# Attention steps, gate steps and accumulating loads set to other times in an fp32 encoder layer, with branch A's operands fetched in ten loads instead of sixteen

## The chip, the cores and the metric

The kernel runs on one core of one Trainium2 chip. The metric is the device time of one execution in microseconds (us), as the median of three runs. Steps, pairs and engines are named as in the program: PE is the matrix engine, DVE the vector engine, ACT the scalar engine, POOL GpSimd, and SP the engine that issues most DMAs.

## The reference

One encoder layer on x of 512 tokens by 2048 channels, fp32. The normed input h goes through one combined projection, whose columns feed a sparse attention (branch A, 8 heads of 128, with a learned top-k key choice), a retention (branch B, 8 heads of 128) and two sigmoid merge gates. Each branch is multiplied by a SiLU gate, projected to 2048 channels, gate-merged, projected once more and added to x; a small gated projection of p and a last norm follow.

```python
a = dsa_mixer(...) * silu(gate_a)          # gate_a, gate_b: columns of the combined projection
b = retention_mixer(...) * silu(gate_b)
merged = sigmoid(g_a) * (a @ w_a) + sigmoid(g_b) * (b @ w_b)
x = x + merged @ w_o
```

## The kernel before

**Products.** An fp32 product is made from two fp32r parts of each operand: a high part, which ACT copies off (`wh`, line 176), and a low part, which DVE subtracts (`wl`, line 183). Weights arrive as raw tiles through SP (line 150). Where a raw tile must hold the sum of two weight blocks, POOL adds the second block with an accumulating DMA (`add_block`, line 137), or DVE adds two raw tiles (line 185).

**A pair** (`gemm_pair`) makes two output blocks with seven products instead of eight, n = 0 to 6, into four banks: `ps_v`, `ps_p`, `ps_q`, `ps_r`, `ps_p`, `ps_v`, `ps_p`. A bank that is used again has to be copied off first: ACT copies `pv` after n = 0, `e1` after n = 1, `e2` after n = 4 and `e3` after n = 6 (line 279), and DVE makes the four results `e_t` (line 283). So product n = 4 waits for `e1`, and product n = 6 for `e2`. A pair has 112 matmuls and a step every two of them, 56 steps. The pairs of `w_b` are short, with four k blocks instead of eight and 28 steps, and use half-size raw tiles (`half_raws`). A plain `gemm` has 24 matmuls and a step every three.

**Order.** Every engine works its instructions off in program order. The program lays the order down by hand: `later(n, f)` issues f n steps on, and `step` runs what is due between two matmuls. A step set later thus puts its instruction behind others on that engine.

**Stages around the change**, in microseconds of the profile: four pairs for branch B's SiLU gate and three for half of branch A's, to about 945, with POOL adding the results (`gate_pair` with `adder=pool`, line 1004) and ACT taking the SiLU one step after (line 1051 and POOL's product and store, lines 1052 and 1053; for branch A line 1013 with its store in line 1014). Then eight pairs for q and k of the attention heads, to about 1165, one per head. The steps of head h are issued during the next two pairs, by the list `steps` in `attention_head`: logits and their maxima, `exps` (DVE `nm` in line 1107, ACT line 1110), `normalize` (DVE lines 1114 and 1118, ACT line 1120), the transposes of the probabilities on PE (`turn`, line 1129), their high parts `pth` and `p3` (ACT, lines 1135 and 1138) and low parts `ptl` (DVE, line 1143), the products with the values (`outs`, lines 1155 and 1157), and the store of the head. One more gate pair lies ahead of the projection of branch B: six plain blocks of `w_b`, four short pairs, two plain blocks. Its operands `bk` are loaded during that last gate pair and split into parts (lines 847 and 848). The result of a short pair is added by POOL (line 1264), multiplied by the merge gate on DVE and stored by SP (lines 1260 and 1261). Branch A's operands for the projection by `w_a`, which begins at about 1278, are loaded by `a_load`, multiplied by their gate on POOL (line 1229) and split.

Of the kernel before, what the change touches and what calls it, by code (L numbers as in the profile page):

```python
# [34 lines left out]
def block_kernel(tc, xT, pT, posb, posq, w_in, w_v, w_k, w_a, w_b, w_o, w_ple, w_gate,  # L35
# [4 lines left out]
    with contextlib.ExitStack() as ctx:  # L40
# [94 lines left out]
        def add_block(r, b):  # L135
            src, k0 = b
            pool.dma_start(out=raw_tiles[r], in_=src[:, k0:k0 + raws[r][2], :], accum_op=OP.add)  # L137

        def load_to(n):
            need = max((u[0] for u in units[:n]), default=-1) + 1  # L140
            while state["raw"] < need:
                i = state["raw"]
                src, k0, nk, cols, plus = raws[i]
                if nk * cols <= L and i < 4:
                    t = U("wraw4").rearrange("p (a c) -> p a c", c=128)
                elif i in half_raws:
                    t = shared("raw", F32, "wraw", RAW_BUFS)
                else:
                    t = wp.tile([128, 8, 128], F32, name="wraw", tag="wraw", bufs=RAW_BUFS)
                sp.dma_start(view(t, nk, cols), src[:, k0:k0 + nk, :])  # L150
                raw_tiles[i] = t
                if plus is not None:
                    add_block(i, plus)
                state["raw"] += 1

        def split_to(n):
# [43 lines left out]
        def later(n, f):  # L200
            if n <= 0:
                return f()
            tick[1] += 1
            heapq.heappush(soon, (tick[0] + n, tick[1], f))
# [791 lines left out]
        def gate_pair(ids, finish, wide=256, adder=None):  # L996
            t = B("go")
            outs = [t[:, 0:512], t[:, 512:1024]]
            have = [0, 0]

            def done(c0, c1, i, q):
                o = outs[i]
                to = alt(o, q)[:, 4 - wide // 64:, :]
                (adder or dve).tensor_add(to, fit(c0, to), fit(c1, to))  # L1004
                have[i] += 1
                if have[i] == 2:
                    later(1, lambda: finish(i, o))

            gemm_pair(ids, Xh, done, wide=wide)

# [51 lines left out]
        def attention_head(h):  # L1062
# [61 lines left out]
            def turn(i):  # L1124
                ps = E["pt", i] = P("ps_pt")
                js = [(0, t) for t in range(4)] if i == 0 else [(1, 1), (1, 2), (1, 3), (3, 3)] if i == 1 \
                    else [(2, 2), (2, 3)]
                for n, (j, t) in enumerate(js):
                    pe.transpose(ps[:, tok(n)], E["bm"][:, TOFF[t] + 128 * j:TOFF[t] + 128 * j + 128], ident)

            def high(i):
                if i == 0:
                    E["p"] = B("pth", F32R), B("ptl", F32R)
                n = (512, 384, 256)[i]
                act.activation(E["p"][0][:, JOFF[i]:JOFF[i] + n], E["pt", i][:, 0:n], AF.Copy)
                if i == 1:
                    E["p3"] = U("p3")
                    act.activation(E["p3"][:, 0:128], E["pt", i][:, 384:512], AF.Copy)

            def low(i):  # L1140
                n = (512, 384, 256)[i]
                c = slice(JOFF[i], JOFF[i] + n)
                dve.tensor_sub(E["p"][1][:, c], E["pt", i][:, 0:n], E["p"][0][:, c].bitcast(F32))
# [4 lines left out]
            def outs(n):  # L1148
                if n == 0:
                    E["po"] = P("ps_o")  # L1150
                po = E["po"]
                for i in range(3 * n, min(3 * n + 3, len(seq))):
                    a, b, j = seq[i]
                    if j == NT - 1:
                        pe.matmul(po[:, 384:], E["v"][0][:, tok(3)].bitcast(F32), E["p3"][:, 0:128], start=False, stop=False)
                    else:
                        pe.matmul(po[:, 128 * j:], E["v"][a][:, tok(j)], E["p"][b][:, JOFF[j]:JOFF[j] + L - 128 * j],
                                  start=(i == 0), stop=(i == len(seq) - 1))
                if n == 3:
                    E["oT"] = U("oT")  # L1160
                    act.activation(E["oT"], po, AF.Copy)

            def store():
                sp.dma_start(od[h], E["oT"])

            steps = [(-30, loads), (-8, mask), (30, values_load)]
            steps += [(n, lambda t=t: logits(t)) for t, n in enumerate((20, 22, 24, 26))]
            steps += [(28, exps), (34, normalize)]
            steps += [(50, lambda i=i: turn(i)) for i in range(3)]
            steps += [(n, lambda i=i: high(i)) for i, n in enumerate((52, 52, 54))]  # L1170
            steps += [(n, lambda i=i: low(i)) for i, n in enumerate((54, 54, 56))]
            steps += [(n, lambda i=i: outs(i)) for i, n in enumerate((65, 65, 69, 69))]
            steps += [(73 + STORE_LAG // 2, store)]
            return done, steps

        for n in range(Z_FIRST):
# [42 lines left out]
        def b_load(h):  # L1219
            t = U("bk")  # L1220
            sp.dma_start(t, bd[h])
            bk[h] = t
            later(25 if h < 5 else 44 - 3 * h + 4 * (h - 5), lambda: bparts.append(split(t, "b", 1)))

        def a_load(h):
            t, z = U("ak"), U("z")
            sp.dma_start(t, od[h])
            sp.dma_start(z, zd[h])
            later(25, lambda: pool.tensor_mul(z, z, t))
            later(29, lambda: aparts.append(split(z, "a", 1)))  # L1230

        for n in range(Z_FIRST, NH // 2):
            if n == NH // 2 - 1:
                for h in range(NH):
                    later(4 + 3 * h, lambda h=h: b_load(h))
            gate_pair(u_az[n], to(zd[2 * n:2 * n + 2], AF.Silu), adder=pool)

        gates = {}
# [13 lines left out]
            later(4, lambda: sp.dma_start(mbs[m], s))  # L1252

        def project_two(m):
            t = U("bo"), U("bo")
            have = [0, 0]

            def finish(i):
                s = gates.pop(m + i)
                dve.tensor_mul(s, t[i], s)  # L1260
                later(8, lambda: sp.dma_start(mbs[m + i], s))

            def done(c0, c1, i, q):
                pool.tensor_add(t[i][:, q], c0, c1)
                have[i] += 1
                if have[i] == 2:
                    later(8, lambda: finish(i))

            gate_load(m + 2)
            gate_load(m + 3)  # L1270
            gemm_pair(u_wb[m], Xb, done, order=range(4))
# [4 lines left out]
        for m in range(16):  # L1276
            if m < B_PAIRS or m >= B_PAIRS + 8:
                project_b(m)
            elif m % 2 == 0:
                if m == B_PAIRS + 4:  # L1280
                    for h in range(NH):
                        later(11 + 4 * h, lambda h=h: a_load(h))
                project_two(m)


# [336 lines left out]
B_PAIRS = 6  # L1622
# [101 lines left out]
```

## Time and profile before

| | |
|---|---|
| median of 3 runs | 1717.44 us (1717.02 to 1718.31) |
| the profiled execution | 1717.35 us, span 1715.5 us, mean granted clock 0.989 |
| PE busy | 1661.2 us, 97% of the span |
| DVE, ACT, POOL busy | 1413.2, 963.7, 350.8 us |
| mean DMA rate | 223 GB/s |

A time in the trace counts from the start of the span. What the program runs outside the span is the difference of the two, 1.85 us. PE's idle time is 54.3 us in all (1715.5 less 1661.2). The granted clock is the share of full speed that PE was given.

### The profile page before, as it was taken

The numbers are of one execution on the slowest core, as the hardware profiler recorded it, in microseconds if no ns is written. First come the engines' busy times: TensorE is split into PE (matmuls) and PEld (weight loads), VectorE is DVE, ScalarE is ACT, GpSimd is POOL, SyncE is SP. The second block draws the span as 40 slices with busy tenths as digits, with TensorE's granted clock in tenths as the row PEclk, the third lists the DMA queues.
The fourth block names the chain that finished last, engine by engine and source line by source line (L and its number), as shares of the span: only waits on it lengthen the run. The fifth ranks groups of instructions, "written<-read, shape, count | busy, mean of one in ns | idle before, by whom it ended". The sixth has DMA issues, their size and how long they took to land.

```text
span 1715.5 us, 26592 instructions
## 1 busy us (share of the span) xinstructions
PE 1661.2 (97%) x9632; PEld 1466.4 (85%) x9632; DVE 1413.2 (82%) x2257; ACT 963.7 (56%) x1501; POOL 350.8 (20%) x355
## 2 busy tenths in 40 slices
PE   9999999999999999999989999998889999999998
PEld 7999998888888888888778888887668888888897
DVE  8789887888988889888886767678687888899895
ACT  6556666555555555554445655556344445477673
POOL 3011111111111111113443101115350033311211
PEclk9999999999999999999999999999999999999999
DMA  8779888787887887878879888776777689998873
GB/s 295 262 237 249 207 207 209 198 218 173 229 225 179 233 225 172 238 202 215 208 184 225 233 231 189 215 203 211 210 275 245 179 224 293 275 321 228 226 236 128
DMA packets 144163, 382.19 MB, mean 223 GB/s; under 512 B 15648, under 2 KB 30112, under 8 KB 144032
## 3 DMA queue, kind: packets, MB, share of 16 engines
q1 hardware_dynamic: 106528, 261.20, 43.6%
q0 software_dynamic: 29872, 106.44, 34.5%
q10 hardware_dynamic: 7632, 12.85, 2.1%
q8 instruction: 76, 1.25, 0.3%
q14 instruction: 55, 0.45, 0.1%
HBM read 331.28 MB, written 49.15 MB: 222 GB/s over the span
## 4 chain that ended last, share of the span: by engine, by line
PE 75%; DVE 10%; issue 5%; ACT 4%; DMA 3%; POOL 2%; SPq 1%; ACTq 0%; POOLq 0%; DVEq 0%
PE ps_p L319 26%; PE ps_v L319 17%; PE ps_r L319 8%; PE ps_q L319 8%; DVE wl L183 4%; PE ps_vn L720 3%; PE ps_w L239 2%; PE ps_w L240 2%; PE ps_w L238 2%; ACT wh L176 1%; DMA wraw<-w_b 1%; POOL go L1004 1%; DVE e_t L283 1%; DVE isc L768 1%; DMA wraw<-w_in 1%
## 5 line engine op out<-in xcount | busy, mean ns | idle before, releaser
L183 DVE TENSOR_TENSOR wl<-wraw,wh 128x1024 fp32r<-128x1024 f32 (+1 forms) x521 | 623.4, 1202 | 189.8 <-ACT wh L176 186.6
L176 ACT ACTIVATE wh<-wraw 128x1024 fp32r<-128x1024 f32 (+2 forms) x520 | 522.8, 1016 | 288.2 <-DVE wraw L185 148.1
L137 POOL DMA_DIRECT2D wraw<-w_in x141 | 125.3, 922 | 805.0 <-DVE wl L183 346.2
L319 PE MATMUL ps_p<-hs,wh 128*128 128x512 f32 (+1 forms) x752 | 188.3, 392 | 0.0
L279 ACT ACTIVATE e<-ps_p 128x512 f32<-128x512 f32 (+1 forms) x195 | 115.0, 590 | 120.7 <-PE ps_p L319 115.6
L319 PEld LDWEIGHTS ps_p<-hs,wh 128*128 128x128 f32 x752 | 135.4, 190 | 24.0 <-issue 1.2
L319 PE MATMUL ps_p<-hs,wl 128*128 128x256 f32 (+1 forms) x752 | 111.8, 290 | 20.5 <-ACT e L279 15.4
L319 PEld LDWEIGHTS ps_p<-hs,wl 128*128 128x128 f32 x752 | 99.8, 196 | 24.0 <-ACT e L279 17.0
L319 PE MATMUL ps_r<-hs,wh 128*128 128x512 f32 (+1 forms) x376 | 98.6, 397 | 7.5 <-ACT wh L176 7.5
L319 PE MATMUL ps_p<-ha,wh 128*128 128x512 f32 (+1 forms) x376 | 95.4, 391 | 0.0
L319 PE MATMUL ps_v<-ha,wh 128*128 128x512 f32 (+1 forms) x376 | 92.9, 388 | 0.0
L319 PE MATMUL ps_v<-hs,wh 128*128 128x512 f32 (+1 forms) x376 | 92.2, 387 | 0.0
L319 PE MATMUL ps_q<-ha,wh 128*128 128x512 f32 (+1 forms) x376 | 92.1, 386 | 0.0
L319 PEld LDWEIGHTS ps_r<-hs,wh 128*128 128x128 f32 x376 | 68.1, 191 | 19.6 <-ACT wh L176 8.5
L319 PEld LDWEIGHTS ps_q<-ha,wh 128*128 128x128 f32 x376 | 70.2, 188 | 14.0 <-ACT wh L176 0.3
L319 PEld LDWEIGHTS ps_v<-hs,wh 128*128 128x128 f32 x376 | 70.3, 188 | 13.8
L319 PEld LDWEIGHTS ps_v<-ha,wh 128*128 128x128 f32 x376 | 69.7, 188 | 13.1
L185 DVE TENSOR_TENSOR wraw<-wraw 128x1024 f32<-128x1024 f32 (+1 forms) x65 | 77.5, 1193 | 2.2
L319 PEld LDWEIGHTS ps_p<-ha,wh 128*128 128x128 f32 x376 | 67.3, 189 | 11.6 <-ACT wh L176 0.4
L283 DVE TENSOR_TENSOR e_t<-ps_p,pv 128x512 f32<-128x512 f32 (+1 forms) x59 | 40.2, 681 | 30.7 <-ACT e L279 28.4
L720 PE MATMUL ps_vn<-wh,hh 128*128 128x296 f32 (+1 forms) x192 | 62.6, 331 | 0.6 <-DVE wh L174 0.4
L720 PE MATMUL ps_vn<-wh,hl 128*128 128x296 f32 (+1 forms) x192 | 62.2, 329 | 0.0
(451 smaller groups left out, 3605.8 us busy)
## 6 DMA issues: line engine op xcount, KB each, us to landing
wraw<-w_in SPq DMA_DIRECT2D x192, 512.0 KB, 4.9
wraw<-w_in POOLq DMA_DIRECT2D x141, 512.0 KB, 7.6
wraw<-w_o SPq DMA_DIRECT2D x32, 512.0 KB, 6.8
wraw<-w_o POOLq DMA_DIRECT2D x24, 512.0 KB, 7.4
wraw<-w_gate SPq DMA_DIRECT2D x24, 512.0 KB, 6.4
wraw<-w_gate POOLq DMA_DIRECT2D x18, 512.0 KB, 6.5
wraw<-w_a SPq DMA_DIRECT2D x16, 512.0 KB, 6.0
rl<-rr SPq DMA_DIRECT2D x24, 256.0 KB, 6.0
```

The lines of the kernel that those rows point to most:

```text
L137: pool.dma_start(out=raw_tiles[r], in_=src[:, k0:k0 + raws[r][2], :], accum_op=OP.add)
L176: act.activation(h, raw, AF.Copy)
L183: dve.tensor_sub(l, raw, h.bitcast(F32))
L185: dve.tensor_add(raw, raw, view(raw_tiles[plus], nk, cols))
L238: pe.matmul(o, h[:, k, w], a, start=(s == order[0]), stop=False)
L239: pe.matmul(o, h[:, k, w], b, start=False, stop=False)
L240: pe.matmul(o, l[:, k, w], a, start=False, stop=(s == order[-1]))
L279: act.activation(E[n], src, AF.Copy)
L283: f(t, x, y)
L319: pe.matmul(to, w[:, k], x, start=(n < 4 and part == parts[0] and k == order[0]), stop=(part == parts[1] and k == order[-1]), skip_group_c ...
L720: pe.matmul(pss[t], x[:, tok(t)], w[:, k], start=(s == 0 and n < NT * len(run) and x is a and w is h), stop=(s == KT - 1 and x is b))
L768: dve.match_replace(out=a, in_to_replace=m8, in_values=a, imm_value=-3.39e38)
```

## The change

The same instructions are issued at other steps, apart from the loads and products of branch A's operands.

- `add_block` of a short pair's raw tile comes 16 steps behind the load of that tile, where it followed at once.
- With `adder=pool`, the SiLU comes 16 steps behind its sum instead of one.
- In attention, `exps`, `normalize`, the transposes, their parts, `outs` and the store come 4 to 11 steps later.
- The product of a head with its SiLU gate moves into attention for heads 0 to 5: a load of the gate, and POOL's product ahead of the store. `a_load` then fetches one tile for these heads, and two for heads 6 and 7: ten loads of 256 KB instead of sixteen, one head every 10 steps from the first short pair on, and split during the last plain blocks of `w_b`.
- Branch B's operands are loaded and split earlier, and the product of a short pair with its merge gate comes 20 steps behind its sum instead of 8.

```diff
-                    add_block(i, plus)
+                    later(16 if i in half_raws else 0, lambda i=i, plus=plus: add_block(i, plus))
...
-                    later(1, lambda: finish(i, o))
+                    later(16 if adder else 1, lambda: finish(i, o))
...
+            def z_load():
+                if h < 2 * Z_FIRST:
+                    E["z"] = U("z")
+                    sp.dma_start(E["z"], zd[h])
+
+            def gate():
+                if h < 2 * Z_FIRST:
+                    pool.tensor_mul(E["oT"], E["z"], E["oT"])
...
-            steps += [(28, exps), (34, normalize)]
-            steps += [(50, lambda i=i: turn(i)) for i in range(3)]
-            steps += [(n, lambda i=i: high(i)) for i, n in enumerate((52, 52, 54))]
-            steps += [(n, lambda i=i: low(i)) for i, n in enumerate((54, 54, 56))]
-            steps += [(n, lambda i=i: outs(i)) for i, n in enumerate((65, 65, 69, 69))]
-            steps += [(73 + STORE_LAG // 2, store)]
+            steps += [(33, exps), (44, normalize)]
+            steps += [(54, lambda i=i: turn(i)) for i in range(3)]
+            steps += [(n, lambda i=i: high(i)) for i, n in enumerate((56, 56, 58))]
+            steps += [(n, lambda i=i: low(i)) for i, n in enumerate((58, 58, 60))]
+            steps += [(n, lambda i=i: outs(i)) for i, n in enumerate((69, 69, 73, 73))]
+            steps += [(48, z_load), (77, gate), (92, store)]
...
-            later(25 if h < 5 else 44 - 3 * h + 4 * (h - 5), lambda: bparts.append(split(t, "b", 1)))
+            later(26 + h if h < 3 else 40 - h, lambda: bparts.append(split(t, "b", 1)))
...
-            t, z = U("ak"), U("z")
+            t = U("ak")
             sp.dma_start(t, od[h])
-            sp.dma_start(z, zd[h])
-            later(25, lambda: pool.tensor_mul(z, z, t))
-            later(29, lambda: aparts.append(split(z, "a", 1)))
+            if h >= 2 * Z_FIRST:
+                z = U("z")
+                sp.dma_start(z, zd[h])
+                later(26, lambda: pool.tensor_mul(t, z, t))
+            later(112 + 1 + 2 * h - 10 * h, lambda: aparts.append(split(t, "a", 1)))
...
-                    later(4 + 3 * h, lambda h=h: b_load(h))
+                    later(2 + h if h < 3 else 3 * h - 1, lambda h=h: b_load(h))
...
-                    later(8, lambda: finish(i))
+                    later(20, lambda: finish(i))
...
-                if m == B_PAIRS + 4:
+                if m == B_PAIRS:
                     for h in range(NH):
-                        later(11 + 4 * h, lambda h=h: a_load(h))
+                        later(10 * h, lambda h=h: a_load(h))
```

On ACT, in the second half of the pair that follows a head's own, the order before is this. Line 1110 is the head's exponentials, line 1120 its normalization, `e2` the copy that product n = 6 of the running pair waits for, and `wh` a weight's high part.

```order
L1110 ACTIVATE bm_10360,sums_10247<-bm_10360,nm_10629 128x512
L176 ACTIVATE wh_10647<-wraw_10284 128x1024
L1120 ACTIVATE bm_10360<-bm_10360,ri_10655 128x128
L1120 ACTIVATE bm_10360<-bm_10360,ri_10655 128x256
L1120 ACTIVATE bm_10360<-bm_10360,ri_10655 128x384
L279 ACTIVATE e2_10673<-ps_p_10497 128x512
```

The same stretch of ACT in the change:

```order
L176 ACTIVATE wh_10643<-wraw_10284 128x1024
L1110 ACTIVATE bm_10360,sums_10247<-bm_10360,nm_10648 128x128
L1110 ACTIVATE bm_10360,sums_10247<-bm_10360,nm_10648 128x256
L1110 ACTIVATE bm_10360,sums_10247<-bm_10360,nm_10648 128x384
L1110 ACTIVATE bm_10360,sums_10247<-bm_10360,nm_10648 128x512
L279 ACTIVATE e2_10670<-ps_p_10495 128x512
L176 ACTIVATE wh_10672<-wraw_10502 128x1024
L1120 ACTIVATE bm_10360<-bm_10360,ri_10685 128x128
```

The copy `e2` and a weight's high part now stand ahead of the normalization, and another weight's high part ahead of the exponentials.

On DVE, at the end of that pair and the start of the next, the order before is this. `ptl` are the low parts of the transposed probabilities, `e_t` and `ak` belong to the k of the next head.

```order
L848 TENSOR_TENSOR aql_10707<-aq_10605,aqh_10706 128x512
L1143 TENSOR_TENSOR ptl_10732<-ps_pt_10712,pth_10731 128x512
L1143 TENSOR_TENSOR ptl_10732<-ps_pt_10717,pth_10731 128x384
L1143 TENSOR_TENSOR ptl_10732<-ps_pt_10722,pth_10731 128x256
L283 TENSOR_TENSOR e_t_10751<-ps_p_10497,pv_10528 128x512
L1085 TENSOR_TENSOR ak_10753<-e_t_10751 128x4x64
L283 TENSOR_TENSOR e_t_10755<-ps_r_10500,e3_10749 128x512
L1085 TENSOR_TENSOR ak_10753<-e_t_10755 128x4x64
L183 TENSOR_TENSOR wl_10765<-wraw_10570,wh_10764 128x1024
```

DVE in the change:

```order
L848 TENSOR_TENSOR aql_10712<-aq_10608,aqh_10711 128x512
L283 TENSOR_TENSOR e_t_10752<-ps_p_10495,pv_10530 128x512
L1085 TENSOR_TENSOR ak_10754<-e_t_10752 128x4x64
L283 TENSOR_TENSOR e_t_10756<-ps_r_10498,e3_10750 128x512
L1085 TENSOR_TENSOR ak_10754<-e_t_10756 128x4x64
L183 TENSOR_TENSOR wl_10766<-wraw_10566,wh_10765 128x1024
L1143 TENSOR_TENSOR ptl_10745<-ps_pt_10727,pth_10744 128x512
L1143 TENSOR_TENSOR ptl_10745<-ps_pt_10732,pth_10744 128x384
L848 TENSOR_TENSOR akl_10774<-ak_10754,akh_10773 128x512
L1143 TENSOR_TENSOR ptl_10745<-ps_pt_10737,pth_10744 128x256
```

The three `ptl` have moved behind two `e_t`, two `ak` and a weight's low part.

On SP, in the short pairs of `w_b`, the order before is this. `wraw` are weight loads, `sg` gate loads, and `mbs` the stores of results: those of line 1252 are of plain blocks, those of line 1261 of the first short pair.

```order
L1252 DMA mbs_1542<-sg_12560 128x512
L150 DMA wraw_12749<-w_b 128x512 x2
L150 DMA wraw_12781<-w_b 128x512 x2
L1243 DMA sg_12845<-sgb_1540 128x512
L1243 DMA sg_12847<-sgb_1540 128x512
L150 DMA wraw_12868<-w_b 128x512 x2
L1261 DMA mbs_1542<-sg_12621 128x512
L150 DMA wraw_12901<-w_b 128x512
L1261 DMA mbs_1542<-sg_12683 128x512
L150 DMA wraw_12901<-w_b 128x512
```

SP in the change, where `ak` are the loads of branch A's operands:

```order
L150 DMA wraw_12768<-w_b 128x512 x2
L1236 DMA ak_12792<-od_1180 128x512
L150 DMA wraw_12801<-w_b 128x512 x2
L1236 DMA ak_12827<-od_1180 128x512
L1254 DMA sg_12867<-sgb_1540 128x512
L1254 DMA sg_12869<-sgb_1540 128x512
L1236 DMA ak_12879<-od_1180 128x512
L150 DMA wraw_12891<-w_b 128x512 x2
L1236 DMA ak_12914<-od_1180 128x512
L150 DMA wraw_12923<-w_b 128x512 x2
L1236 DMA ak_12961<-od_1180 128x512
L1273 DMA mbs_1542<-sg_12638 128x512
```

The first short pair's stores have moved behind all loads of the short pairs, and five loads of branch A's operands stand among those.

More of the change, by code (lines that the diff above doesn't have):

```diff
@@ L1254, in project_two @@
         def project_two(m):
-            t = U("bo"), U("bo")
+            o = B("bo")
+            t = o[:, 0:512], o[:, 512:1024]
             have = [0, 0]
```

## The prediction

> **What bounds the kernel now.** I read the page first.
>
> ```profile
> span 1715.5 us, 26592 instructions
> PE 1661.2 (97%) x9632; PEld 1466.4 (85%) x9632; DVE 1413.2 (82%) x2257; ACT 963.7 (56%) x1501; POOL 350.8 (20%) x355
> ```
>
> PE is busy for 97% of the span, and the change leaves its matmuls as they are. All it can give back is the time in which PE waits, or in which it runs at a lower granted clock. The busy times of the four stretches that the change touches come next.
>
> ```profile
> core 0: us, PE busy (x) PEld busy (x) DVE busy (x) ACT busy (x) POOL busy (x), PEclk, DMA share, GB/s
> 780.00:945.00 165.00, 152.29 (x856) 131.86 (x855) 130.98 (x210) 76.62 (x99) 68.76 (x67) 0.99 0.82 211
> 945.00:1170.00 225.00, 209.64 (x1191) 186.88 (x1190) 158.33 (x266) 137.99 (x248) 30.17 (x33) 0.96 0.81 223
> 1170.00:1209.00 39.00, 37.03 (x160) 30.49 (x159) 31.77 (x49) 19.93 (x47) 21.34 (x23) 0.96 0.55 156
> 1209.00:1285.00 76.00, 61.23 (x303) 51.37 (x302) 59.56 (x71) 32.72 (x54) 36.92 (x32) 0.93 0.77 242
> ```
>
> They are the SiLU pairs, attention, the plain blocks of `w_b`, and the short pairs up to the start of `w_a`. PE is idle for 12.7, 15.4, 2.0 and 14.8 us in them (length less busy). The clock costs more: length times (1 less PEclk) gives 1.7, 9.0, 1.6 and 5.3 us. So the stakes are 14.4, 24.4, 3.5 and 20.1 us, 62.4 in all, and 1655 is the floor of what this change could reach. The waits say who holds PE up. In the SiLU pairs:
>
> ```profile
> ACT go L1051 <- POOL go L1004: 35.9, 8, 6.4
> ACT go L1013 <- POOL go L1004: 18.0, 6, 6.4
> PE ps_r L319 <- ACT wh L176: 7.5, 5, 2.0
> PE ps_p L319 <- DVE wl L183: 4.6, 7, 1.3
> ```
>
> ACT stands for 54 us at SiLUs whose sum POOL has not made, and the weights' high parts behind it come late to PE, and through them the low parts. In attention:
>
> ```profile
> PE ps_p L319 <- ACT e L279: 15.4, 8, 2.9
> DVE wl L183 <- ACT wh L176: 58.8, 33, 3.3
> POOL wraw L137 <- DVE wl L183: 141.4, 15, 21.4
> ```
>
> All of PE's waiting there is one wait per pair, for `e2` ahead of product n = 6. The timeline of one pair shows why, and what follows it (the last row is the busy-times view of the four microseconds after the wait).
>
> ```profile
> 974.58 1.26 PE L1129 MATMUL ps_pt<-cs,bm 128*128 128x128 f32 x10
> ...
> 993.70 0.40 ACT L1110 ACTIVATE bm<-bm,nm 128x128 f32<-128x128 f32 x1 [2.90 <-DVE nm L1107]
> ...
> 995.51 1.98 PE L319 MATMUL ps_v<-ha,wh 128*128 128x512 f32 x8
> ...
> 995.90 1.04 ACT L176 ACTIVATE wh<-wraw 128x1024 fp32r<-128x1024 f32 x1
> ...
> 998.38 1.30 ACT L1120 ACTIVATE bm<-bm,ri 128x128 f32<-128x128 f32 x3 [1.44 <-DVE ri L1114]
> 999.59 0.57 ACT L279 ACTIVATE e<-ps_p 128x512 f32<-128x512 f32 x1
> ...
> 1000.22 0.74 PE L319 MATMUL ps_p<-hs,wl 128*128 128x256 f32 x4 [1.78 <-ACT e L279]
> 1000.80 2.21 PE L1129 MATMUL ps_pt<-cs,bm 128*128 128x128 f32 x10
> ...
> 1000.20:1004.20 4.00, 3.98 (x20) 3.89 (x21) 3.02 (x4) 2.57 (x4) 1.42 (x2) 0.59 0.18 70
> ```
>
> ACT idles 1.44 us for the reciprocal, normalizes for 1.30 us, and only then copies `e2`. PE waits 1.78 us, and in this pair runs the next four at a clock of 0.59: the same ten transposes take 2.21 us against 1.26 one pair earlier.
>
> **Attention, what goes.** With `e2` ahead of the normalization, the copy has only the exponentials ahead of it. They began here at 993.70, when their input came, and were done at 995.90, and product n = 4 ends at 995.51, where n = 5 begins: `e2` is made while n = 5 runs, well ahead of n = 6. The eight waits of 15.4 us go, and their 9.0 us of clock.
>
> **Attention, what is late next.** `ptl` has moved behind the next head's k on DVE, and PE's `outs` need it early in the next pair. The durations are in the timeline of before.
>
> ```profile
> 977.97 1.98 PE L319 MATMUL ps_v<-hs,wh 128*128 128x512 f32 x8
> 979.19 1.48 DVE L1143 TENSOR_TENSOR ptl<-ps_pt,pth 128x512 fp32r<-128x512 f32 x3
> 979.72 0.62 ACT L279 ACTIVATE e<-ps_p 128x512 f32<-128x512 f32 x1
> 980.59 0.68 DVE L283 TENSOR_TENSOR e_t<-ps_p,pv 128x512 f32<-128x512 f32 x1
> 980.74 0.40 PE L319 MATMUL ps_p<-ha,wl 128*128 128x256 f32 x2
> 982.71 1.22 DVE L183 TENSOR_TENSOR wl<-wraw,wh 128x1024 fp32r<-128x1024 f32 x1
> 983.85 0.69 DVE L848 TENSOR_TENSOR akl<-ak,akh 128x512 fp32r<-128x512 f32 x1
> ```
>
> The pair starts at T = 977.97, and product n = 1 at T + 2.8. `outs` stand ten matmuls into n = 1 (eight with `wl`, two with `wh`, 1.4 us), and their first `ptl` comes two matmuls of `pth` (0.4 us) later: PE asks for it at T + 4.6. DVE's chain starts from `e3`: 0.9 us to the first `e_t`, 2.1 us to the weight's low part (980.59 to 982.71), 1.1 us for that, and 1.1 for the two `ptl` that PE waits for, 5.2 in all. `e3` began at T + 1.75 before; it now has the third `pth` behind it instead of ahead (0.4 us), and the chain of `aq` in front of it no longer starts from a late `e2`, so I put it between T + 0.7 and T + 1.35. Then `ptl` is there at T + 5.9 to T + 6.6, 1.3 to 2.0 us too late, and the third `ptl`, behind `akl`, takes some tenths more. I take 1.7 us a pair. Seven heads have this; the eighth's `outs` lie among plain blocks. 11.9 us of waiting come back. A slow stretch costs 1.6 us (4.00 times 0.41), so the old waits brought five or six in eight pairs; the new wait is about as long but in two pieces, and I take three of seven, 5 us. Attention gains 24.4 less 16.9, about 7.5 us. If the wait grows to 2.5 with a slow stretch each time, it loses 5 (17.5 and 11.5 against 24.4); without it, it gains all 24.4.
>
> The Trainium skill, "TensorE: Matmul & The Clock Gate", section "Why this matters for your kernels", warns of idle gaps above about 3 us only. By that the new waits would cost no clock. The row above speaks against it, 0.59 behind a wait of 1.78 us.
>
> **What attention also gets.** Six loads of 256 KB, at a DMA share of 0.81, and six products on POOL, which is busy for 30 of 225 us. DVE's operations may stretch beside them, by less than the 58.8 us that it idles for ACT. I cost both at nothing; the cover fails if POOL stands at line 137 when its product is due (a rival below).
>
> **SiLU pairs.** A full pair is seven products of 2.77 us (977.97 to 980.74 above), 19.4 us without attention's work, so 16 of its 56 steps are 5.5 us. A SiLU that came one step behind its sum waited for POOL 3.9 us in the mean (53.9 by 14) and 6.4 at most. Coming 5.5 us later, nearly all of that goes. What keeps some of the 14.4 us is DVE, busy for 131 us in 165: part of the 4.6 us for `wl` is its own load. I leave 3.4 and take 11 (7 to 14).
>
> **Plain blocks of `w_b`.**
>
> ```profile
> PE ps_w L239 <- DVE bl L848: 2.0, 1, 2.0
> ```
>
> The eight splits of branch B come earlier, so this wait and its clock go, 3.5 us (2 to 3.5).
>
> **Short pairs.**
>
> ```profile
> PE ps_p L319 <- ACT e L279: 9.3, 3, 6.8
> PE ps_w L239 <- DVE al L848: 3.1, 1, 3.1
> PE ps_p L319 <- DVE e_t L283: 2.4, 1, 2.4
> POOL wraw L137 <- DMA wraw<-w_b: 13.1, 1, 13.1
> ...
> 1213.04 1.19 SPq L150 DMA_DIRECT2D wraw<-w_b  x2
> 1226.13 0.33 SPq L1261 DMA_DIRECT2D mbs<-sg  x1
> ...
> 1230.21 1.88 POOL L137 DMA_DIRECT2D wraw<-w_b  x2
> 1238.99 0.63 ACT L176 ACTIVATE wh<-wraw 128x512 fp32r<-128x512 f32 x1 [7.96 <-DMA wraw<-w_b]
> 1242.75 1.22 PE L319 MATMUL ps_p<-bs,wl 128*128 128x256 f32 x4 [6.78 <-ACT e L279]
> ```
>
> POOL stood 13.1 us at an accumulating transfer whose tile had not landed, its sums came late, DVE's product with the gate too, and SP stood at that product's store from 1214.2 to 1226.1 with the weight loads behind it. The accumulating transfers then came at 1230.2, landed at 1239, and PE waited 6.78 us. In the change POOL asks 16 short steps (5.5 us) behind the load, the stores stand behind all weight loads, and branch A's splits have left these pairs, which takes the 2.4 and 3.1 with them. It does not all go. A short pair is half of 19.4 us, 9.7, and the chain through it is longer: a high part (0.6), its low part (half of 1.22), the accumulating transfer (8.7 in the rows above), the next high part, low part, sum and high part (2.4) and `e1` (0.6), 12.9 us, or some 2 less where fewer transfers are in flight. I leave 1, 3 and 3 us in the second to fourth pair and 5 us of clock, 12 of the 20.1, and take 8 (4 to 14).
>
> **Sum.** 11 + 7.5 + 3.5 + 8 = 30, and 1717.35 less that is 1687. The profiled execution lies 0.1 us below the median of 1717.44, so no correction is needed.
>
> **Rivals.** (1) `outs` don't wait: ACT reaches `e3` so early that `ptl` is ready. Attention gains all 24.4, and the time is 1670. For it: ACT has 87 us idle in 225. Against it: 5.2 us of DVE work stand between. (2) The short pairs keep their waits, since the chain through the accumulating transfer sets them and the ten loads add to a DMA share of 0.77: 1695. (3) The SiLU's later place does not help, because DVE's load sets the waits: 1698. (4) SP stands at a head's store. The store now waits for POOL's product; if POOL stands at line 137 then (up to 21.4 us, 141.4 in all), SP holds the loads of `w_in` behind it. In the short pairs a hold of 11.9 us became a wait of 6.78, so loads have about 5 us of slack; from there it decides. Six heads with 6.78 us and two slow stretches each, 10, would add 60: 1747, slower. Against it: POOL's product is due at step 77 and the store at 92, at least 5.2 us apart, and the transfer ahead of it waits for a load, not for `wl`. (5) Waits below 3 us cost no clock: the 5 us in attention and the 5 in the short pairs fall away, 1677. Against it stands the row with 0.59.
>
> **How the numbers follow.** My forecast has 0.55, the rivals 0.2, 0.1, 0.05, 0.06 and 0.04. A difference of 0.2%, 3.4 us, is what a measurement of this kernel can tell from none. The single terms at their low ends give 7 - 5 + 2 + 4 = 8, so 1709; rival 1 gives 1670, with 2 us more from the short pairs 1668. The range is 1668 to 1708. Slower has rival 4's 0.06 and 0.01 from low ends together; the same, 0.03; faster, 0.9.
>
> **What would show it.** Right: in the SiLU pairs ACT no longer waits for POOL and PE loses under 4 us; in attention no wait for `e` at n = 6, but one of 1.3 to 2 us for `ptl` at line 1157 in seven pairs; no wait for `bl` or `al`; in the short pairs no SP row at rest for 12 us, and three waits below 4 us. Wrong: PE gapless in attention, a wait of PE for `wh` behind a late `wraw` there, or a wait above 6 us in the short pairs.

## The result, and the profile after

The changed kernel takes 1687.67 us in the median of four runs (1685.51 to 1688.58), against 1717.66 for the kernel before in four runs. The ratio is 0.9824, with a 95% interval of 0.9807 to 0.9841. The forecast was 1687, so the whole came out as predicted. The parts did not all, and one of them came from another cause than the one given.

The head of the page, with the changed kernel's span and PE's busy time:

```profile
span 1686.8 us, 26584 instructions
PE 1654.5 (98%) x9632; PEld 1457.4 (86%) x9632; DVE 1420.1 (84%) x2257; ACT 963.2 (57%) x1501; POOL 352.7 (21%) x355
```

PE is idle for 32.3 us instead of 54.3, and busy for 6.7 us less with the same matmuls. So 22 us come from waits, and the rest from the clock and from what a wait costs beside its length (shown below). The profiled execution took 1688.58 us, the longest of the four.

To see where, I set marks: the same matmuls in both kernels, with the start of the first and of the last of a group. First the kernel before (the first logits of a head, the plain blocks of `w_b`, the blocks of `w_a`):

```profile
L1100 PE MATMUL ps_l<-ak,aq x16: 270/272/274, 961.0 to 1151.1; 128*128 128x128 f32 x16
L238 PE MATMUL ps_w<-bh,wh x64: 388/389/628, 1170.6 to 1272.7; 128*128 128x512 f32 x64
L238 PE MATMUL ps_w<-ah,wh x128: 388/389/628, 1273.4 to 1364.7; 128*128 128x512 f32 x128
```

The same marks in the changed kernel:

```profile
L1100 PE MATMUL ps_l<-ak,aq x16: 270/272/275, 950.8 to 1140.7; 128*128 128x128 f32 x16
L238 PE MATMUL ps_w<-bh,wh x64: 387/389/400, 1156.0 to 1248.7; 128*128 128x512 f32 x64
L238 PE MATMUL ps_w<-ah,wh x128: 389/389/389, 1249.4 to 1335.7; 128*128 128x512 f32 x128
```

The lead is 10.2 us at the first logits, 14.6 at the first block of `w_b`, 24.0 at the first of `w_a` and 29.0 at the last of `w_a`. Of the first, 0.6 us were there before the SiLU pairs (the last matmul of line 899, ahead of them, starts at 785.9 before and at 785.3 after). So the SiLU pairs gave 9.6, attention and the gate pair behind it 4.4, and `w_b` with `w_a` 14.4. The longest matmuls of the last two groups (628 ns before, 400 and 389 after) show that no slow stretch, some microseconds at a lower granted clock, touches these plain blocks any more.

The waits of the SiLU pairs after:

```profile
ACT go L1051 <- POOL go L1004: 6.7, 6, 1.8
PE ps_p L319 <- DVE wl L183: 4.3, 7, 0.7
PE ps_q L319 <- DVE wl L183: 1.0, 1, 1.0
```

ACT stands 6.7 us at these SiLUs where it stood 35.9, and PE no longer waits for `wh` at `ps_r`. What is left, 5.9 us with 0.6 for a `wh` at `ps_p`, is nearly all a wait for DVE's low parts. In attention:

```profile
PE ps_o L1157 <- DVE ptl L1143: 11.0, 14, 1.5
ACT bm L1120 <- DVE ri L1114: 11.5, 8, 1.4
```

ACT still stands for the reciprocal, but nobody waits for that now. SP stands at the stores of six heads for POOL's new product:

```profile
SPq L1173 <- POOL oT L1170: 11.3, 6, 2.4
```

That delays no weight load enough to reach PE, which waits for no weight in attention.

The wait for `e2` is gone, and one for `ptl` has taken its place, twice in each of seven pairs. The timeline of the start of a pair shows the chain:

```profile
992.85 1.99 PE L319 MATMUL ps_v<-hs,wh 128*128 128x512 f32 x8
...
993.97 0.61 ACT L279 ACTIVATE e<-ps_p 128x512 f32<-128x512 f32 x1
994.61 0.69 DVE L283 TENSOR_TENSOR e_t<-ps_p,pv 128x512 f32<-128x512 f32 x1 [0.82 <-ACT e L279]
...
996.74 1.22 DVE L183 TENSOR_TENSOR wl<-wraw,wh 128x1024 fp32r<-128x1024 f32 x1
...
997.05 0.57 PE L1157 MATMUL ps_o<-pth,av 128*128 128x512 f32 x2
...
997.88 1.15 DVE L1143 TENSOR_TENSOR ptl<-ps_pt,pth 128x512 fp32r<-128x512 f32 x2
...
999.08 0.44 PE L1157 MATMUL ps_o<-ptl,av 128*128 128x384 f32 x1 [1.46 <-DVE ptl L1143]
...
999.36 0.34 PE L1157 MATMUL ps_o<-pth,avl 128*128 128x384 f32 x1
...
999.54 0.42 DVE L1143 TENSOR_TENSOR ptl<-ps_pt,pth 128x256 fp32r<-128x256 f32 x1
...
1000.01 0.45 PE L1157 MATMUL ps_o<-ptl,av 128*128 128x256 f32 x1 [0.20 <-DVE ptl L1143]
```

With T = 992.85, `e3` begins at T + 1.1, the two `ptl` are there at T + 6.2, and PE waits 1.46 and 0.20 us. Two neighbouring pairs of the changed kernel, from one T to the next, in the view of busy times:

```profile
1020.86:1047.11 26.25, 24.80 (x145) 21.51 (x144) 19.44 (x33) 15.87 (x31) 5.35 (x5) 1.00 0.86 228
1047.11:1075.13 28.02, 26.36 (x145) 22.76 (x144) 19.88 (x33) 16.53 (x32) 4.85 (x5) 0.94 0.81 215
```

Three of the seven pairs, every second one, have a slow stretch (0.94) and are 1.8 us longer. In the short pairs and the plain blocks behind them:

```profile
PE ps_p L319 <- ACT e L279: 6.3, 4, 2.6
ACT wh L176 <- DMA wraw<-w_b: 13.2, 5, 5.6
POOL wraw L137 <- DVE wl L183: 17.3, 3, 10.6
```

Four waits of 0.6, 2.6, 1.8 and 1.2 us are left for `e1`, and none for `al` or `e_t`. POOL no longer stands for a load.

### The profile page after: what moved, and what is told of

The parts are those of the page before. It is cut to its first block, busy times and chain, and to the rows that moved or that the text cites. A ratio compares the mean times of both kernels' runs of the same rounds, so it can differ in the third digit from the quotient of the medians.

```text
span 1686.8 us, 26584 instructions
## 1 busy us (share of the span) xinstructions
PE 1654.5 (98%) x9632; PEld 1457.4 (86%) x9632; DVE 1420.1 (84%) x2257; ACT 963.2 (57%) x1501; POOL 352.7 (21%) x355
## 4 chain that ended last, share of the span: by engine, by line
PE 79%; DVE 8%; ACT 4%; DMA 3%; issue 3%; POOL 2%; POOLq 0%; SPq 0%; ACTq 0%; DVEq 0%
PE ps_p L319 25%; PE ps_v L319 16%; PE ps_q L319 9%; PE ps_r L319 9%; PE ps_vn L720 6%; DVE wl L183 4%; DMA wraw<-w_b 2%; PE ps_w L239 2%; PE ps_w L238 2%; PE ps_w L240 2%; ACT wh L176 1%; DVE e_t L283 1%; DVE isc L768 1%; DVE m L767 1%; ACT bm L1110 1%
## 5 line engine op out<-in xcount | busy, mean ns | idle before, releaser
L183 DVE TENSOR_TENSOR wl<-wraw,wh 128x1024 fp32r<-128x1024 f32 (+1 forms) x521 | 630.4, 1215 | 164.3 <-ACT wh L176 156.1
L319 PE MATMUL ps_p<-hs,wl 128*128 128x256 f32 (+1 forms) x752 | 106.3, 283 | 4.9 <-DVE wl L183 4.3
L185 DVE TENSOR_TENSOR wraw<-wraw 128x1024 f32<-128x1024 f32 (+1 forms) x65 | 82.4, 1267 | 2.2
L319 PEld LDWEIGHTS ps_p<-ha,wh 128*128 128x128 f32 x376 | 68.3, 193 | 11.5 <-ACT wh L176 0.4
L720 PE MATMUL ps_vn<-wl,hh 128*128 128x296 f32 (+1 forms) x192 | 62.2, 329 | 0.0
```

What stands on the lines that cost most here:

```text
L183: dve.tensor_sub(l, raw, h.bitcast(F32))
L185: dve.tensor_add(raw, raw, view(raw_tiles[plus], nk, cols))
L319: pe.matmul(to, w[:, k], x, start=(n < 4 and part == parts[0] and k == order[0]), stop=(part == parts[1] and k == order[-1]), skip_group_c ...
L720: pe.matmul(pss[t], x[:, tok(t)], w[:, k], start=(s == 0 and n < NT * len(run) and x is a and w is h), stop=(s == KT - 1 and x is b))
```

## The experiments

Every ratio is to the kernel before in the same session, with its 95% interval; that kernel's median there was 1715.37, 1717.12 and 1717.43 us in the three sessions. The first three tell what holds PE in attention.

**The products with the values five steps later.**

```diff
-            steps += [(n, lambda i=i: outs(i)) for i, n in enumerate((69, 69, 73, 73))]
-            steps += [(48, z_load), (77, gate), (92, store)]
+            steps += [(n, lambda i=i: outs(i)) for i, n in enumerate((74, 74, 78, 78))]
+            steps += [(48, z_load), (82, gate), (92, store)]
```

> The changed kernel with the products with the values five steps later (74, 74, 78, 78 instead of 69, 69, 73, 73) and the gate product at 82. Theory: PE's 14 waits of 11.0 us for ptl are a matter of order only, ptl comes 1.7 us after PE asks; five steps are 2.2 us, so these waits go to under 1 us, and with them the three slow stretches of the clock in attention (about 1.4 us each). Expected 1687.7 less 11 less 4, about 1673, within 1670 to 1677. Rival: PE is held up in attention by DVE's or ACT's load as such, and the wait moves on to the next product (a wait for wh, wl or e in the same pairs); then within 3 us of 1687.7.

Measured 1667.47 us, ratio 0.9717 (0.9702 to 0.9733). A pair's busy times:

```profile
1014.77:1039.02 24.25, 24.25 (x146) 21.62 (x144) 18.81 (x33) 16.10 (x32) 4.81 (x5) 1.00 0.93 250
```

PE has no gap in the pair. The periods from one head pair to the next are 24.24 or 24.25 us, and no slow stretch is left. The wait was a matter of order: DVE and ACT have room for all of it. The gain is 19.6 us at the first block of `w_b`: 11.0 of waits, some 4.7 of slow stretches (three pairs with 26.36 us of PE's time instead of 24.80), and some 3.9 of breaks (seven pairs with 24.80 instead of 24.25), which I had left out. The same products with the values show where a break costs:

```profile
997.01 0.56 PE L1157 MATMUL ps_o<-pth,av 128*128 128x512 f32 x2
997.41 0.34 PE L1157 MATMUL ps_o<-ptl,av 128*128 128x384 f32 x1
997.58 0.34 PE L1157 MATMUL ps_o<-pth,avl 128*128 128x384 f32 x1
```

Without a wait, the first `ptl` product starts 0.40 us after the two of `pth`, and the next 0.17 us on. In the timeline of the change, the two of `pth` take their whole 0.57 us before the wait begins, and the product behind the wait is followed after 0.28 us. That is 0.3 us beside the 1.46 us of this wait, and the second wait costs about as much again.

**The three `ptl` ahead of the weight's low part.**

```diff
-            steps += [(n, lambda i=i: high(i)) for i, n in enumerate((56, 56, 58))]
-            steps += [(n, lambda i=i: low(i)) for i, n in enumerate((58, 58, 60))]
+            steps += [(n, lambda i=i: high(i)) for i, n in enumerate((56, 56, 57))]
+            steps += [(n, lambda i=i: low(i)) for i, n in enumerate((57, 57, 57))]
```

> The changed kernel with the third high part at step 57 instead of 58 and all three low parts at 57 instead of 58, 58, 60, so that on DVE the three ptl stand ahead of the weight's low part and not behind it. Theory (DVE's queue ahead of ptl makes the wait): 1.1 us of the chain of 5.2 us goes from in front of ptl, the wait per head falls from 1.67 to 0.4 to 0.7 us in two pieces, no slow stretch of the clock is left; 1687.7 less 8 less 4, about 1676, within 1672 to 1680. Rival: ACT is late with the high parts, and ptl waits for them wherever it stands; then the waits keep 1.2 us or more and the time stays above 1683.

Measured 1673.59 us, ratio 0.9751 (0.9731 to 0.9771).

```profile
PE ps_o L1157 <- DVE ptl L1143: 2.6, 7, 0.4
```

Seven waits of 0.4 us are left of fourteen with 11.0 us, and the pairs are 24.9 us long, all alike. Moving one 1.1-us operation of DVE behind the `ptl` takes 1.1 us from the longer wait and ends the shorter one. ACT's last `pth` begins 2.6 us behind the start of the pair here as in the change, so DVE's queue ahead of the `ptl` is what PE waited for, and not ACT's high parts.

**Attention's steps as before, the rest changed.**

```diff
-            steps += [(33, exps), (44, normalize)]
+            steps += [(28, exps), (34, normalize)]
-            steps += [(54, lambda i=i: turn(i)) for i in range(3)]
+            steps += [(50, lambda i=i: turn(i)) for i in range(3)]
...
-            steps += [(n, lambda i=i: outs(i)) for i, n in enumerate((69, 69, 73, 73))]
+            steps += [(n, lambda i=i: outs(i)) for i, n in enumerate((65, 65, 69, 69))]
```

> The changed kernel with the attention steps of before (exponentials 28, normalization 34, transposes 50, parts 52 to 56, products 65 to 69), the gate product and its loads and the later store kept. Theory: attention's own change gained only 4 us, since one wait took the place of the other: the waits for e at 1.78 us come back in the pairs, those for ptl go, and the time is 1692, within 1689 to 1696. Rival: the whole gain in attention is in these steps (24 us forecast as the stake): then above 1700; or the gate product and the loads in attention cost something, then below 1689.

Measured 1691.22 us, ratio 0.9856 (0.984 to 0.9873).

```profile
PE ps_p L319 <- ACT e L279: 19.5, 11, 2.4
```

The waits for `e` are back (15.2 us of these 19.5 lie in attention, the rest in the short pairs), those for `ptl` are gone, and the difference to the change is 0.0032 of 1717, 5.5 us, with intervals that touch. The new steps are worth little as they stand, as theory one had it.

**The SiLU one step behind its sum.**

```diff
-                    later(16 if adder else 1, lambda: finish(i, o))
+                    later(1, lambda: finish(i, o))
```

> The changed kernel with the SiLU one step behind its sum as before, all else kept. Theory: ACT stands at the SiLUs again, PE waits 12 to 13 us in the SiLU pairs instead of 5.9, one slow stretch comes back: 1687.7 plus 8 to 10, about 1697. Rival: DVE's load alone sets these waits, and the time stays within 3 us of 1687.7.

Measured 1699.12 us, ratio 0.9901 (0.9884 to 0.9917), 0.0077 or 13 us above the change.

```profile
ACT go L1051 <- POOL go L1004: 35.9, 8, 6.4
PE ps_r L319 <- ACT wh L176: 7.5, 5, 2.0
...
L1100 PE MATMUL ps_l<-ak,aq x16: 270/272/275, 959.5 to 1149.5; 128*128 128x128 f32 x16
```

ACT's 35.9 us and PE's 7.5 are those of before again, and the first logits come at 959.5, 8.7 us later than in the change. That is the forecast's mechanism, though the slow stretch that I expected back did not come: the granted clock is 1.00 over the SiLU pairs here. What else lies in the 13 us is not in this stage. From the first block of `w_b` to that of `w_a` this run took 1.2 us more, the profiled executions lie 11.1 us apart, and the rest is within the intervals.

The next seven take apart the short pairs and what feeds them.

**The accumulating transfer right behind its load.**

```diff
-                    later(16 if i in half_raws else 0, lambda i=i, plus=plus: add_block(i, plus))
+                    later(0, lambda i=i, plus=plus: add_block(i, plus))
```

> The changed kernel with the accumulating transfer of a short pair's tile issued right behind its load, as before, all else kept. Theory: POOL stands at that transfer again for up to 13 us with the short pairs' sums behind it, e_t's tiles and the next accumulating transfers come late, and PE waits 3 to 6 us more in the short pairs; ratio to before 0.9845 to 0.986 (the change alone had 0.9824). Rival: what held SP was the early store alone, which is still late here; then the ratio stays at 0.982 to 0.984.

Measured 1687.13 us, ratio 0.9822 (0.9807 to 0.9836): no difference. The waits of POOL and PE in the short pairs:

```profile
POOL wraw L137 <- DMA wraw<-w_b: 10.4, 1, 10.4
...
PE ps_p L319 <- ACT e L279: 5.1, 2, 4.7
```

POOL stands for a load for 10.4 us again, and PE loses 5.1 us instead of 6.3. The rival is right: POOL's hold costs nothing that can be measured while the store stands late.

**The product with the gate 8 steps behind the sum.**

```diff
-                    later(20, lambda: finish(i))
+                    later(8, lambda: finish(i))
```

> The changed kernel with the product of a short pair with its gate 8 steps behind the sum instead of 20, so that the store stands ahead of later weight loads on SP again, all else kept. Theory: with POOL no longer held, the sums come in time and SP is held by 1 to 3 us only; PE loses 1 to 3 us more in the short pairs, ratio 0.983 to 0.9845. Rival (the early store was the cause): the wait of 6 to 7 us comes back, ratio 0.985 to 0.988.

Measured 1695.05 us, ratio 0.9872 (0.9856 to 0.9888), 0.0048 or 8.2 us above the change. SP's and PE's rows:

```profile
1200.38 0.33 SPq L1236 DMA_DIRECT2D ak<-od  x1
1208.84 0.33 SPq L1273 DMA_DIRECT2D mbs<-sg  x1
1209.26 0.38 SPq L150 DMA_DIRECT2D wraw<-w_b  x1
...
1208.84 1.22 PE L319 MATMUL ps_p<-bs,wl 128*128 128x256 f32 x4 [3.17 <-DVE sg L1272]
```

SP stands at the store from 1200.7 to 1208.8 with weight loads behind it, though POOL does not stand for a load here. So SP's hold does not need POOL's, and the theory's 1 to 3 us for it were wrong. The time is the rival's, but its wait of 6 to 7 us did not come back: PE waits 0.6, 3.2, 3.0 and 1.9 us in the short pairs, 8.6 us instead of 6.3. The stage from the first block of `w_b` to that of `w_a` is 6.8 us longer; the other 4.4 us are busy time of the same matmuls, at a clock of 0.93 instead of 0.98. The profile puts the 3.17 us down to DVE's product with the gate, which ended at 1208.81, but ACT's copy `e1` ended at 1208.78, so the row doesn't tell which of the two PE needed. The early product with its store is the cause. Which of its two parts, the product on DVE or the store on SP, this run can't say, since the edit moves both.

**Both undone.**

```diff
-                    later(16 if i in half_raws else 0, lambda i=i, plus=plus: add_block(i, plus))
+                    later(0, lambda i=i, plus=plus: add_block(i, plus))
...
-                    later(20, lambda: finish(i))
+                    later(8, lambda: finish(i))
```

> The changed kernel with both undone: the accumulating transfer right behind its load, and the product with the gate 8 steps behind the sum. Theory: the late transfer is worth nothing by itself (its undoing alone had ratio 0.9822), and the early store costs 8.5 us (0.9872); together they cost what the early store costs, ratio 0.986 to 0.988. Rival: POOL's hold makes the early store's hold longer, and the two together cost 11 us or more, ratio 0.9885 to 0.991.

Measured 1698.41 us, ratio 0.989 (0.9873 to 0.9906), with waits of 0.7, 4.9, 3.2 and 0.7 us in the short pairs. The ratio lies in the rival's range, 0.0066 or 11 us above the change. But its interval reaches into the theory's range and overlaps with that of the run before, so whether POOL's hold adds to the early store's cost is not settled.

**The product 20 steps behind the sum, alone in the kernel before.**

```diff
-                    later(8, lambda: finish(i))
+                    later(20, lambda: finish(i))
```

> The kernel before with one part of the change alone: the product of a short pair with its gate 20 steps behind the sum instead of 8. Theory (the early store held SP): the wait of 6.8 us in the short pairs shrinks to under 4, the time falls by 4 to 9 us, ratio 0.995 to 0.9977. Rival: POOL's hold at the accumulating transfer (13 us) makes that wait by itself, and the ratio is 0.998 to 1.002.

Measured 1710.08 us, ratio 0.9957 (0.9942 to 0.9972).

```profile
L238 PE MATMUL ps_w<-ah,wh x128: 387/389/396, 1267.7 to 1354.8; 128*128 128x512 f32 x128
...
PE ps_p L319 <- ACT e L279: 6.7, 3, 3.2
PE ps_w L239 <- DVE al L848: 0.3, 1, 0.3
```

The longest wait of 6.78 us has become 3.2. The wait for `al` has gone from 3.1 to 0.3 with the sixteen loads of before in their place: in the kernel before, SP stood at a store from 1233.0 to 1243.1 with fourteen of them behind it. This one number, 8 to 20, brings 7 of the 30 us.

**Sixteen loads at the old place.**

```diff
-                if m == B_PAIRS:
+                if m == B_PAIRS + 4:
                     for h in range(NH):
-                        later(10 * h, lambda h=h: a_load(h))
+                        later(11 + 4 * h, lambda h=h: a_load(h))
...
-            steps += [(48, z_load), (77, gate), (92, store)]
+            steps += [(92, store)]
```

(`a_load` is that of the kernel before.)

> The changed kernel with branch A's operands as before: no gate product in attention, sixteen loads 4 steps apart from the third short pair on, products and splits in the short pairs and behind. Theory: POOL's eight products and DVE's eight splits lie in the last short pair and the plain blocks again, so the waits for al (3.1) and e_t (2.4) come back with one slow stretch, and the loads crowd the last two pairs: 6 to 9 us more than the change, ratio 0.986 to 0.988. Rival: these splits had room once the short pairs are not late; then 0.982 to 0.984.

Measured 1686.71 us, ratio 0.982 (0.9806 to 0.9835): no difference. PE's waits in this stretch:

```profile
PE ps_p L319 <- ACT e L279: 8.9, 5, 3.2
...
PE ps_w L239 <- DVE al L848: 0.3, 1, 0.3
```

The rival is right on the waits. The ten loads, which stand in the title, and the gate products in attention are worth nothing measurable in the whole. In the parts they are not nothing. In this profile attention, without the six loads and products, takes 199.3 us from the first logits to the first block of `w_b`, at a clock of 1.00, where the change took 205.2 at 0.98; `w_b` then takes 2.9 us more and `w_a` 0.8. So what the edit gave at the end it took in attention, mostly by slow stretches: none in this run's head pairs, three in those of the change.

**Branch A's loads ahead of the short pairs, on top of the later products with the values.**

```diff
+        for h in range(2 * Z_FIRST):
+            later(8 * h, lambda h=h: a_load(h, 112 + 49 + 2 * h - 8 * h))
         for m in range(16):
...
-                    for h in range(NH):
+                    for h in range(2 * Z_FIRST, NH):
```

> The kernel with the later products with the values (ratio 0.9717 to before) and in addition branch A's loads for heads 0 to 5 moved from the short pairs into the plain blocks ahead of them, where DMA has room (share 0.5 to 0.8 against 1.06 in the short pairs); splits stay where they are. Theory: what is left of PE's waiting in the short pairs (about 5 us and one slow stretch) comes from accumulating transfers that land late because the ten loads compete; with four of them left it falls to 2 to 3 us, ratio 0.969 to 0.9705. Rival: the chain through the accumulating transfer is that long by itself, and nothing changes, ratio 0.971 to 0.9725.

Measured 1670.51 us, ratio 0.9724 (0.9709 to 0.9738), against 0.9717 (0.9702 to 0.9733) without this: the same. PE's waits in the short pairs are 7.5 us instead of 5.0. So competition from these loads is not what sets them.

**Branch B's operands as before.**

```diff
-            later(26 + h if h < 3 else 40 - h, lambda: bparts.append(split(t, "b", 1)))
+            later(25 if h < 5 else 44 - 3 * h + 4 * (h - 5), lambda: bparts.append(split(t, "b", 1)))
...
-                    later(2 + h if h < 3 else 3 * h - 1, lambda h=h: b_load(h))
+                    later(4 + 3 * h, lambda h=h: b_load(h))
```

> The changed kernel with branch B's operands loaded and split at the steps of before, all else kept. Theory: PE's wait of 2.0 us for bl in the first plain block of w_b comes back with a slow stretch, 3 to 4 us more than the change (ratio 0.9824 alone, 0.982 in the run with sixteen loads): ratio 0.984 to 0.9848. Rival: that wait followed from the 2.9 us wait ahead of it, which is gone; then the ratio stays at 0.982 to 0.983.

Measured 1688.83 us, ratio 0.9835 (0.9821 to 0.985), between the two expectations.

```profile
PE ps_w L239 <- DVE bl L848: 0.9, 1, 0.9
```

The wait for `bl` comes back with 0.9 us, not 2.0, and without a slow stretch, so 2.0 us is not a fixed price of the old splits. The wait of 2.9 us ahead of it does not set it either: the run with the product 20 steps behind the sum, alone in the kernel before, is the same program up to there, has the same wait of 2.9 us, and waits 0.5 us for `bl`. What makes it 0.5 or 2.0 is not shown. The time itself can't be told from the change's.

**A version that goes further.** Key choice, which runs on DVE in the background of the SiLU pairs, every 11 steps instead of 9, with the later products with the values:

```diff
-BG_RATES = (3, 3, 4, 10, 8, 9)
+BG_RATES = (3, 3, 4, 10, 8, 11)
```

> The kernel with the later products with the values (ratio 0.9717), and the background work of key choice on DVE every 11 steps in the SiLU pairs instead of every 9. Theory: what is left of PE's waiting in the SiLU pairs, 5.9 us for wl and wh, is DVE's load; with the same work spread over the last SiLU pairs, which have no wait, it falls to 2 to 4 us, ratio 0.9693 to 0.971. Rival: a wait of PE for wl follows from the place of these operations and not from their density, and the work now reaches into attention; ratio 0.9715 to 0.975.

Measured 1663.69 us, ratio 0.9687 (0.9673 to 0.9702), 24 us below the change. Against the kernel with the later products alone it is 5 us less, with intervals that touch.

```profile
PE ps_p L319 <- DVE wl L183: 1.4, 3, 0.6
PE ps_q L319 <- DVE wl L183: 0.5, 1, 0.5
```

The low parts' waits fall from 5.3 to 1.9 us, and the one for `wh` is gone. What the SiLU pairs had kept was DVE's load. The largest waits of PE that are left are three in the short pairs, 5.8 us together.

## Why the prediction was right, point by point

- **SiLU pairs.** Forecast 11, measured 9.6. The mechanism held (the run with the SiLU at once). I left 3.4 us, and 5.9 of waits alone stayed, above my sign of under 4; spreading DVE's background work took 4 of them away.
- **Attention, what goes.** All eight waits for `e2` went. The stake was sized rightly: from the first logits to the first block of `w_b` the kernel before takes 209.6 us, and the kernel with the later products 185.7, 23.9 less; I had 24.4.
- **Attention, what is late next.** The new wait was called at its place and size: asked for at T + 4.6 (4.8 measured), there at T + 5.9 to 6.6 (6.2 measured), 11.9 us in seven pairs (11.0 measured).
- **What the new waits cost beside their length** was the term that I mis-sized. The stage takes 205.2 us, 19.5 above 185.7, so some 8.5 us lie there beside the 11.0 of waits. The slow stretches came as forecast, in three of seven pairs, some 4.7 us against my 5. What I put at nothing are the breaks themselves, about 0.55 us in each of the seven pairs, 3.9 us (24.80 us busy against 24.25, both at a clock of 1.00). Attention gained 4.4 instead of 7.5.
- **What attention also gets** I cost at nothing. That is not borne out: without the six loads and products (the run with sixteen loads) this stage takes 5.9 us less in the profile.
- **Short pairs with the plain blocks and `w_a`.** Forecast 3.5 + 8, measured 14.4, and the step on the cause failed in three places. POOL's hold was not what started the chain: undone alone, it costs nothing that can be measured. Branch A's splits leaving the pairs is not what took the 3.1 us for `al`: with them back, it stays at 0.3. And the 2.0 us for `bl` came back as 0.9 with the old splits. The early product with its store was the cause, worth 7 to 8 us: SP's queue held the weight loads and branch A's loads alike. I had named that hold, but as one link of four. The three waits that I left there, 1, 3 and 3 us, came as 0.6, 2.6, 1.8 and 1.2, since the chain through the accumulating transfer stays; neither less competition (7.5 us instead of 5.0) nor an earlier transfer (5.1 instead of 6.3, the time the same) ended them.
- **Rivals.** (1) did not occur but is what the later products give, 1667 against my 1670. (2) was half right: the chain does set waits, but shorter ones. (3) fell. (4) stopped short of its point: SP does stand at the heads' stores for POOL (row above), but 2.4 us at most, under the 5 us of slack. (5) fell: waits of 1.46 us brought slow stretches.
- **The sum.** That it came out at 1687 is in part luck: the SiLU pairs and attention gave 4.5 us less than forecast, and the last stages 2.9 more. Two slips in the working changed nothing: seven slow stretches of 1.6 us are 11.2 us and not 11.5, and the low ends give 1709, 1 us outside the range.

The parts undone one at a time add up to about 29 of the 30 us by ratio (13 for the SiLU, 5.5 for attention's steps, 8 for the product's 20 steps, 2 for branch B's operands, 0 twice), with some 2.5 us of uncertainty in each. One edit is not among them: the change also puts the two results `bo` of a short pair into one tile instead of two, which no run undoes alone.

## What to carry to other kernels

When a step is moved out of the way of one wait, follow every instruction that now stands behind something on each in-order queue, down to the engine that asks for it next: here a wait of 1.78 us became two of 1.66 us together, and five more steps for the last link were worth 18 us, where the whole move was worth 5.5. Where a queue also issues loads, look at the stores on it that wait for their data, before looking at what made the data late: a product and store 12 steps later were worth 7 us here by themselves. When several edits go together, undo each alone, and look at each stage: the ten loads of the title were worth nothing in the whole, since they took in one stage what they gave in another.

## What the runs showed of the hardware

A short wait costs more than its length. The matmuls of a head pair take 24.25 us of PE's time without a wait, 24.80 in a pair with waits of 1.45 us in two pieces at a granted clock of 1.00, and 26.36 in one with 1.66 us at 0.94. Waits of 0.4 us (24.9-us pairs) brought no slow stretch. Length alone does not decide it: the first head pair of the change has waits of 1.67 us at a clock of 1.00, and in its short pairs the wait of 2.64 us (in the first row) brought no slow stretch, the one of 1.83 us (in the second) did.

```profile
1205.00:1215.00 10.00, 7.36 (x43) 6.29 (x43) 8.68 (x13) 6.62 (x12) 5.25 (x6) 1.00 0.73 196
1215.00:1225.00 10.00, 8.17 (x39) 6.77 (x39) 7.68 (x12) 4.91 (x9) 3.39 (x6) 0.85 1.06 316
```

What decides it, no run here shows. The Trainium skill, "TensorE: Matmul & The Clock Gate", section "Why this matters for your kernels", sets the limit for idle gaps at about 3 us; in this kernel the clock fell behind gaps of half that, so the measurement decides.

DVE's low part of a weight, 1.22 us in most rows, can take much longer beside POOL's operations. DVE and POOL in the SiLU pairs of the changed kernel:

```profile
824.44 1.40 DVE L183 TENSOR_TENSOR wl<-wraw,wh 128x1024 fp32r<-128x1024 f32 x1
...
826.61 3.05 DVE L183 TENSOR_TENSOR wl<-wraw,wh 128x1024 fp32r<-128x1024 f32 x1
...
826.98 1.58 POOL L1052 TENSOR_TENSOR go<-go,y 128x512 f32<-128x512 f32 x1
```

The Trainium skill, "GPSIMD Engine Reference", section "1. Specifications", says that GpSimd shares its SBUF interfaces with VectorE and contends with DVE instructions that read two SBUF inputs; the 1.8 us by which the second one is longer are near POOL's 1.58. But the first, beside two sums of POOL (824.0 to 826.4), is only 0.2 us longer, and no run here moved POOL's operations away from DVE's to show it alone.
